# Inverse softmax sums as a diagonal in the transposing products, and half of the modulation products moved behind the SSD's residual sums

## The chip, the cores and the metric

The kernel runs on one core of a Trainium2 chip. The metric is the device time of one execution in microseconds; the time before is the median of three runs. A profiled execution gives the trace from which the rows are read. The engines are named as there: PE (TensorE matmul), PEld (its weight load), DVE (VectorE), ACT (ScalarE), POOL (GpSimd), SP (SyncE, which here only issues DMAs).

## The reference

One layer of an encoder for 1024 positions of width 1024, in fp32. The parts that the change touches are the modulation, the softmax of the chunked attention, and the places where the modulation is used:

```python
mod = (c_act @ w_ada[l] + b_ada[l])[:, None, :]
sh_m, sc_m, g_m, sh_f, sc_f, g_f = jnp.split(mod, 6, axis=-1)
h = rmsnorm(x, norm_mix_w[l]) * (1 + sc_m) + sh_m
z, xbc, dt_raw, q, k, v = jnp.split(h @ w_in[l], IN_SPLITS, axis=-1)
...
# attention: 8 heads of 64, chunks of 64, own chunk and 8 before it
scores = jnp.where(valid, scores + bias[:, None], jnp.finfo(jnp.float32).min)
p = jax.nn.softmax(scores, axis=-1).astype(v.dtype)
o = jnp.einsum('bhcqk,bckhd->bcqhd', p, vb)
...
x = x + g_m * (jnp.concatenate([y_ssd, y_att], axis=-1) @ w_out[l])
h = rmsnorm(x, norm_ffn_w[l]) * (1 + sc_f) + sh_f
x = x + g_f * conv_ffn(h, w_up[l], ffn_conv_w[l], w_down[l])
```

`mod` has 6 x 1024 = 48 x 128 values; each group of 128 is the product of a 128 x 1024 block of the transposed `w_ada` with the activated `c`. The first 16 (`sh_m`, `sc_m`) are needed before anything else, `g_m` with the output projection, `sc_f` and `sh_f` before the FFN's input, and `g_f` only in the last stage.

## The kernel before

**Numbers.** Large products are made from fp32 values split in a rounded high part and a rest (`split`: ACT writes the high part, DVE the low one), and three products of the parts (`mm3`, lines 56 to 58).

**Stages.** First the mixing norm, its 16 modulation products and the projections of head pairs 0 and 1 (to about 104 us). Then attention, four pairs of heads (`attention(0)` to `attention(3)`); the projections of pairs 2 and 3 run inside pairs 1 and 2, and the SSD's convolutions already fill PE during pair 3. Then the eight convolved groups (`conv_silu`, B, C and x), the `z` projection in two halves of eight row tiles, the SSD in eight chunks of 128 rows (`ssd_chunk`), with the output projection (`wout_tile`) of six of the eight row tiles behind it, the FFN's input (`h_raw`, `sums`), the FFN's up products, and its down products.

**Attention.** For each query tile of 128 rows and each of two heads `attn_scores` makes the scores on PE (L306), adds the bias and takes the row's extreme on DVE (L318), takes the exponential and its sums on ACT (L321), inverts the sums on DVE (L323) and scales the row block with them on DVE (L324, up to 128 x 640). `attn_pv` then turns blocks of 128 x 128 with PE transposes against the identity (L350, L353), splits the turned bank (L65 on ACT, L66 on DVE) and multiplies with the values (L361, L362). The first query tile has one block, later ones up to five: 30 blocks for a head.

**Modulation.** `mod_col` loads a block of 512 KB (L112, on SP's queue) and reduces it with the row of `c` on DVE (L113, which also has a short read-out of its sum). 16 products run in the first stage. The other 32 run with the convolutions and `z`: three for each of the eight groups, for `g_m`, `sc_f` and `sh_f` (`mods`, three buffers), and eight for `g_f` after them, in buffers that the `x` groups also use. `mod_scale` and `mod_shift` turn each column into the FFN norm's factor and offset (`affn`, `bffn`; L168, L170, L174). `row_of` turns eight columns into a row on all partitions: DVE writes a diagonal (L120), PE multiplies it with ones (L123), ACT copies (L124). It runs in the second half of `z` for `g_m` (which is folded into `w_out`, L513) and for `g_f`; the latter row goes to DRAM (`gfd`) and returns in the last stage.

**SSD and output projection.** One row tile at a time, DVE combines the chunk's parts, scales it (L705), PE turns it (L708), DVE puts it into `xs` (L709), ACT and DVE split it (`yh`, `yl`), PE multiplies with `w_out`, and DVE adds the input's rows, loaded on SP's queue (L735), to it (L747). `norm_row` then makes the FFN norm's factor as a diagonal (L759), which `h_raw` multiplies with (L797): plain fp32 products of blocks of 128 x 128, where attention has transposes.

**What sets the order.** Each engine runs its instructions, and SP its loads, in a fixed order. The framework derives it, from the code and from its own estimate of when operands are there; so the order differs from the code's and can move at places that were not edited. `issue_after(i)` keeps an instruction behind `i` in that order.

Of the kernel before, what the change touches and what calls it, by code (L numbers as in the profile page):

```python
# [10 lines left out]
F32 = mybir.dt.float32  # L11
F32R = mybir.dt.float32r
AF = mybir.ActivationFunctionType
ALU = mybir.AluOpType
# [13 lines left out]
FOLD = (0, 1, 0, 1)  # L28
PRST = 4
MTB = 3  # L30
GP, GPL = {0: (0,1), 2: (2,)}, ()
XL = (3, 4, 5, 6)
KH = NF // 2
# [12 lines left out]
def tile_block(ctx: ExitStack, tc: tile.TileContext, x, crep, pk, w_ada, w_first, w_ft, w_z,  # L46
# [39 lines left out]
    def stat(n=1):  # L86
        if stc[0] + n > 64:
            stc[0] = 0
        a = st1[:, stc[0]:stc[0] + n]
        stc[0] += n  # L90
        return a
# [16 lines left out]
        rawc[0] += 1  # L108
        return raws[:, rawc[0] % 2, 0:n]

    def mod_col(ft, t):
        nc.sync.dma_start(t, w_ada[ft])  # L112
        V.tensor_tensor_reduce(out=t, in0=t, in1=rowa, scale=1.0, scalar=0.0,  # L113
                               op0=ALU.mult, op1=ALU.add, accum_out=modc[:, ft:ft + 1])

    def row_of(cols, dst, psp, tag, bufs, ones, tmp):
        for hh in range(2):
# [45 lines left out]
    affn = const.tile([P, 8], F32, name="affn")  # L163
    bffn = const.tile([P, 8], F32, name="bffn")

    def mod_scale(dst, sc, nw, kt):
        t = stat()
        V.tensor_tensor(t, modc[:, sc + kt:sc + kt + 1], pkt[:, B_ADA + sc + kt:B_ADA + sc + kt + 1],  # L168
                        ALU.add)
        V.scalar_tensor_tensor(dst[:, kt:kt + 1], t, 1.0, pkt[:, nw + kt:nw + kt + 1],  # L170
                               op0=ALU.add, op1=ALU.mult)

    def mod_shift(dst, sh, kt):
        V.tensor_tensor(dst[:, kt:kt + 1], modc[:, sh + kt:sh + kt + 1],  # L174
                        pkt[:, B_ADA + sh + kt:B_ADA + sh + kt + 1], ALU.add)
# [120 lines left out]
    def attn_scores(p, i, bt):  # L296
        d = qk[p]
        j0 = max(0, i - 4)
        n = (i - j0 + 1) * P
        off = (j0 - (i - 4)) * P  # L300
        parts = [(0, n)] if n <= 512 else [(0, 320), (320, 320)]
        st = [s_tile(), s_tile()]
        for h in range(2):
            for pi, (a, w) in enumerate(parts):
                for ti, kn in enumerate(("kh", "kl")):
                    T.matmul(st[h][:, 512 * pi:512 * pi + w], d["q"][h][:, i * P:(i + 1) * P],  # L306
                             d[kn][h][:, j0 * P + a:j0 * P + a + w], start=ti == 0, stop=ti == 1)
        res = []
        for h in range(2):
            pt_ = p_tile()  # L310
            nm, rs = stat(), stat()
            if len(parts) == 1:
                src, bsl, dst = st[h][:, 0:n], bt[h][:, off:off + n], pt_[:, 0:n]
            else:
                src = st[h].rearrange("p (a b) -> p a b", a=2)[:, :, 0:320]
                bsl = bt[h].rearrange("p (a b) -> p a b", a=2)
                dst = pt_.rearrange("p (a b) -> p a b", a=2)
            V.tensor_tensor_reduce(out=dst, in0=src, in1=bsl, scale=-1.0, scalar=3e38,  # L318
                                   op0=ALU.add, op1=ALU.min, accum_out=nm)
# [4 lines left out]
            V.tensor_scalar(pv_, pv_, rr, None, op0=ALU.mult)  # L324
            res.append(pt_)
        return res

    def attn_pv(p, u, h, p0, p1):
# [12 lines left out]
        while done < nb:  # L341
# [5 lines left out]
            tps = tp_tile()  # L347
            for (j, c0, n), o in bank:
                if c0 == 0:
                    T.transpose(tps[:, o:o + P], p0[:, (j - lo0) * P:(j - lo0 + 1) * P], ident)  # L350
                if c0 + n == 256:
                    o1 = o + P - c0
                    T.transpose(tps[:, o1:o1 + P], p1[:, (j - lo1) * P:(j - lo1 + 1) * P], ident)  # L353
            k = ptc[0] % 3
            ptc[0] += 1
            hi, lo = pt[:, 2 * k, 0:used], pt[:, 2 * k + 1, 0:used]
# [116 lines left out]
    def mods(kt):  # L473
        mod_col(G_M + kt, mt_tile())
        mod_col(SC_F + kt, mt_tile())
        mod_scale(affn, SC_F, NFFN, kt)
        mod_col(SH_F + kt, mt_tile())
        mod_shift(bffn, SH_F, kt)

    for g in range(2):  # L480
        conv_silu(4 + g, bt_[g], th512)
# [96 lines left out]
            T.matmul(dps[:, 64 * i:64 * i + 64], m, sm["adt"], start=True, stop=True)  # L578
        A.activation(ex3, dps[:, 0:192], AF.Exp)

    for kt in range(KT):
        mod_col(G_F + kt, bcp.tile([P, S], F32, tag="rm", bufs=2, name="mt"))
    def hb(n, c):
        return sm[n][:, c * 8:c * 8 + 8].unsqueeze(2).to_broadcast([P, 8, 64])

# [42 lines left out]
    for st in range(NT):  # L628
# [103 lines left out]
    def wout_tile(st):  # L732
        xr = [wop.tile([P, 512], F32, tag="xr", bufs=2, name="xr") for _ in range(2)]
        for dh in range(2):
            nc.sync.dma_start(xr[dh], x[st * P:(st + 1) * P, halves[dh]])  # L735
        ps = [ps2b.tile([P, 512], F32, tag="wo", bufs=PB[0], name="wops") for _ in range(2)]
        for part in range(2):
            yh = wop.tile([P, 4, P], F32R, tag="yh", bufs=3, name="yh")
# [5 lines left out]
                    mm3(ps[dh], yh[:, k, :], yl[:, k, :], w[0], w[1], part == 0 and k == 0,  # L744
                        part == 1 and k == 3)
        for dh in range(2):
            V.tensor_tensor(x1[dh][:, st, :], ps[dh], xr[dh], ALU.add)  # L747
            nc.scalar.dma_start(x1d[st * P:(st + 1) * P, halves[dh]], x1[dh][:, st, :])

    dg = {}  # L750

# [541 lines left out]
```

## Time and profile before

| | |
|---|---|
| runs | 1271.11, 1270.83, 1270.24 us (median 1270.83) |
| profiled execution | 1271.27 us, span 1269.6 us, mean granted clock of PE 0.977 |
| busy over the span | PE 1189.2 us (94%), DVE 984.6 (78%), ACT 560.4 (44%), POOL 108.0 (9%) |
| 32 modulation products with the convolutions and z | 41.6 us of DVE, 512 KB each |
| 64 scalings of the probabilities | 29.6 us of DVE |

A row that groups instructions has: line, engine, operation, output<-inputs, shapes, count | busy us, mean ns of one | idle time of the engine before them and what ended it. A tile's row has the shortest, median and longest duration in ns. A row of the timeline begins with start and duration in us. PEclk is the share of the TensorE clock that was granted.

### The profile page before, as it was taken

How to read it: one execution, taken by the hardware profiler on the slowest of the kernel's cores; microseconds unless marked ns; L12 is line 12 of the kernel's file. 1: busy time of each engine (PE TensorE's matmuls, PEld its weight loads, DVE VectorE, ACT ScalarE, POOL GpSimd, SP SyncE). 2: the span in 40 equal slices, each digit the busy share in tenths (PEclk: the TensorE clock that was granted, in tenths of full speed). 3: DMA queues.
4: the chain of work that ended last, by engine and by line, in shares of the span. 5: the costliest groups of instructions: out<-in, count | busy, mean ns of one | idle time of the engine just before them, and what ended most of it. 6: DMA issues, size and time to landing. Idle time of an engine off the chain costs nothing.

```text
span 1269.6 us, 15525 instructions
## 1 busy us (share of the span) xinstructions
PE 1189.2 (94%) x5786; PEld 991.8 (78%) x5786; DVE 984.6 (78%) x1533; ACT 560.4 (44%) x917; POOL 108.0 (9%) x114
## 2 busy tenths in 40 slices
PE   5898999989979979999889999999999999999995
PEld 3686788778869868888668888888888888888884
DVE  7836666694698886764999988888988879856976
ACT  4525555573324453423744444443444445443443
POOL 1300011101220242220000000000000000000002
PEclk9998899999989989999999999999999999999998
DMA  8712111201564422112213322323322295834433
GB/s 331 258 29 65 38 51 54 62 17 34 183 226 140 166 83 67 54 55 90 69 67 124 119 80 90 110 100 124 119 81 89 79 321 208 303 110 143 158 124 132
DMA packets 57835, 150.85 MB, mean 119 GB/s; under 512 B 5793, under 2 KB 5921, under 8 KB 56353
## 3 DMA queue, kind: packets, MB, share of 16 engines
q1 hardware_dynamic: 50704, 125.49, 29.4%
q10 hardware_dynamic: 7056, 24.38, 4.8%
q8 instruction: 45, 0.74, 0.2%
q14 instruction: 30, 0.24, 0.1%
HBM read 116.56 MB, written 29.10 MB: 115 GB/s over the span
## 4 chain that ended last, share of the span: by engine, by line
PE 76%; DVE 14%; DMA 4%; ACT 3%; issue 2%; POOL 1%; SPq 0%; DVEq 0%; POOLq 0%; ACTq 0%
PE dn L57 5%; PE dn L56 5%; PE dn L58 5%; PE uY L56 5%; PE uY L58 5%; PE uY L57 5%; PE uZ L58 3%; PE uZ L56 3%; PE uZ L57 3%; PE uX L56 3%; PE uX L58 3%; PE uX L57 3%; PE acc L56 3%; PE acc L57 3%; PE acc L58 2%
## 5 line engine op out<-in xcount | busy, mean ns | idle before, releaser
L56 PE MATMUL dn<-w 128*128 128x512 f32 x308 | 111.9, 389 | 0.0
L57 PE MATMUL dn<-w 128*128 128x512 f32 x308 | 111.9, 389 | 0.0
L58 PE MATMUL dn<-w 128*128 128x512 f32 x308 | 103.3, 389 | 0.0
L65 ACT ACTIVATE w<-ya 128x1024 fp32r<-128x1024 f32 (+1 forms) x44 | 41.8, 950 | 95.6 <-PE uY L58 87.1
L764 POOL TENSOR_TENSOR st<-st,mhalf 128x1 f32<-128x1 f32 x16 | 12.4, 777 | 678.2 <-DVE st L763 678.2
L56 PEld LDWEIGHTS dn<-w 128*128 128x128 f32 x308 | 57.8, 188 | 12.1
L57 PEld LDWEIGHTS dn<-w 128*128 128x128 f32 x308 | 57.8, 188 | 12.0
L58 PEld LDWEIGHTS dn<-w 128*128 128x128 f32 x308 | 57.8, 188 | 11.9
L65 ACT ACTIVATE w<-xs 128x1024 fp32r<-128x1024 f32 (+1 forms) x44 | 41.8, 951 | 43.5 <-PE uY L58 37.5
L56 PE MATMUL s<-hth,wh 128*128 128x512 f32 x128 | 51.7, 404 | 8.8 <-DVE st L168 8.0
L66 DVE TENSOR_TENSOR pt<-tp,pt 128x512 fp32r<-128x512 f32 (+2 forms) x72 | 42.0, 595 | 17.7 <-ACT pt L65 17.2
L318 DVE CUSTOM_DVE_ANT_0 p<-s,bias 128x640 f32<-128x640 f32 (+4 forms) x64 | 40.8, 649 | 18.4 <-PE s L306 10.1
L321 ACT ACTIVATE p<-p,st 128x640 f32<-128x640 f32 (+4 forms) x64 | 44.1, 691 | 19.8 <-DVE st L318 18.7
L66 POOL TENSOR_TENSOR wl<-raws,wh 128x1024 fp32r<-128x1024 f32 x14 | 36.5, 2612 | 189.3 <-ACT wh L65 145.9
L906 DVE SCALAR_TENSOR_TENSOR a<-cv,pkt,a 128x1023 f32<-128x1023 f32 (+1 forms) x40 | 51.0, 1276 | 0.1
L57 PE MATMUL s<-htl,wh 128*128 128x512 f32 x128 | 51.0, 398 | 0.0
L58 PE MATMUL s<-hth,wl 128*128 128x512 f32 x128 | 50.9, 398 | 0.0
L66 DVE TENSOR_TENSOR w<-ya,w 128x1024 fp32r<-128x1024 f32 (+1 forms) x44 | 47.7, 1085 | 4.0 <-ACT w L65 4.0
L113 DVE CUSTOM_DVE_ANT_0 mt<-mt,rows 128x1024 f32<-128x1024 f32 x32 | 41.6, 1301 | 10.6 <-DMA mt<-in_w_ada_dram 10.6
L906 DVE SCALAR_TENSOR_TENSOR a<-cg,pkt,a 128x1023 f32<-128x1023 f32 (+1 forms) x40 | 49.6, 1276 | 0.0
L65 ACT ACTIVATE pt<-tp 128x512 fp32r<-128x512 f32 (+2 forms) x72 | 36.3, 523 | 28.8 <-PE tp L350 12.3
L66 DVE TENSOR_TENSOR w<-xs,w 128x1024 fp32r<-128x1024 f32 (+1 forms) x44 | 47.6, 1083 | 0.0
(407 smaller groups left out, 3607.6 us busy)
## 6 DMA issues: line engine op xcount, KB each, us to landing
mt<-in_w_ada_dram SPq DMA_DIRECT2D x32, 512.0 KB, 3.8
gz<-a ACTq DMA_DIRECT2D x10, 1024.0 KB, 5.3
adat<-in_w_ada_dram SPq DMA_DIRECT2D x16, 512.0 KB, 6.5
ya<-in_w_up_dram SPq DMA_DIRECT2D x10, 768.0 KB, 4.0
xs<-in_w_up_dram SPq DMA_DIRECT2D x10, 768.0 KB, 4.1
raws<-in_w_ft_dram SPq DMA_DIRECT2D x14, 512.0 KB, 3.5
gy<-a ACTq DMA_DIRECT2D x10, 512.0 KB, 2.6
qk<-in_x_dram SPq DMA_DIRECT2D x8, 512.0 KB, 6.7
```

The lines of the kernel that those rows point to most:

```text
L56: T.matmul(ps, lh, rh, start=start, stop=False, skip_group_check=more)
L57: T.matmul(ps, lh, rl, start=False, stop=False, skip_group_check=more)
L58: T.matmul(ps, ll, rh, start=False, stop=stop, skip_group_check=more)
L65: i = A.activation(hi, src, AF.Copy) if ehi is A else ehi.tensor_copy(hi, src)
L66: return i, elo.tensor_tensor(lo, src, f32(hi), ALU.subtract)
L113: V.tensor_tensor_reduce(out=t, in0=t, in1=rowa, scale=1.0, scalar=0.0, op0=ALU.mult, op1=ALU.add, accum_out=modc[:, ft:ft + 1])
L318: V.tensor_tensor_reduce(out=dst, in0=src, in1=bsl, scale=-1.0, scalar=3e38, op0=ALU.add, op1=ALU.min, accum_out=nm)
L321: A.activation(pv_, pv_, AF.Exp, scale=-1.0, bias=nm, accum_out=rs)
L764: G.tensor_tensor(r, ms, mhalf[:, 0:1], ALU.pow)
L906: V.scalar_tensor_tensor(a[:, j:S], c[:, 0:S - j], w[2 - j], a[:, j:S], op0=ALU.mult, op1=ALU.add)
```

## The change

**Diagonal.** `attn_scores` no longer scales the probabilities. It scales the identity by the inverse sums to a diagonal `dr` (128 x 128, six buffers), on ACT for the first head of a pair and on DVE for the second, and returns it with the block. `attn_pv` multiplies each block with its diagonal in a plain fp32 product in place of the transpose; the result is the turned and scaled block.

**Modulation.** `mods` keeps `g_m` and `sc_f`. The 16 products for `sh_f` and `g_f` go into the loop over the six row tiles: none at the first, three at each of the next four, four at the last. Their load stands behind the load of the tile's input rows, and their reduction behind the tile's residual sum; they have two buffers. Factor and offset are now made for all eight columns at once, and the row of `g_f` and its copy to DRAM stand behind the loop.

```diff
+DRB = 6
+LATE = (0, 0, 3, 6, 9, 12, 16)
...
-    def mod_col(ft, t):
-        nc.sync.dma_start(t, w_ada[ft])
-        V.tensor_tensor_reduce(out=t, in0=t, in1=rowa, scale=1.0, scalar=0.0,
-                               op0=ALU.mult, op1=ALU.add, accum_out=modc[:, ft:ft + 1])
+    def mod_col(ft, t, at=None):
+        sp_, v_ = at or (None, None)
+        with tc.issue_after(sp_) if sp_ else ExitStack():
+            nc.sync.dma_start(t, w_ada[ft])
+        with tc.issue_after(v_) if v_ else ExitStack():
+            V.tensor_tensor_reduce(out=t, in0=t, in1=rowa, scale=1.0, scalar=0.0,
+                                   op0=ALU.mult, op1=ALU.add, accum_out=modc[:, ft:ft + 1])
...
             rr = stat()
             V.reciprocal(rr, rs)
-            V.tensor_scalar(pv_, pv_, rr, None, op0=ALU.mult)
-            res.append(pt_)
+            dr = ptp.tile([P, P], F32, tag="dr", bufs=DRB, name="dr")
+            if h == 0:
+                A.activation(dr, ident, AF.Copy, scale=rr)
+            else:
+                V.tensor_scalar(dr, ident, rr, None, op0=ALU.mult)
+            res.append((pt_, dr))
...
-                    T.transpose(tps[:, o:o + P], p0[:, (j - lo0) * P:(j - lo0 + 1) * P], ident)
+                    k = slice((j - lo0) * P, (j - lo0 + 1) * P)
+                    T.matmul(tps[:, o:o + P], p0[0][:, k], p0[1], start=True, stop=True)
...
-                    T.transpose(tps[:, o1:o1 + P], p1[:, (j - lo1) * P:(j - lo1 + 1) * P], ident)
+                    T.matmul(tps[:, o1:o1 + P], p1[0][:, k], p1[1], start=True, stop=True)
...
     def mods(kt):
         mod_col(G_M + kt, mt_tile())
         mod_col(SC_F + kt, mt_tile())
-        mod_scale(affn, SC_F, NFFN, kt)
-        mod_col(SH_F + kt, mt_tile())
-        mod_shift(bffn, SH_F, kt)
...
-    for kt in range(KT):
-        mod_col(G_F + kt, bcp.tile([P, S], F32, tag="rm", bufs=2, name="mt"))
...
-        if st == ROWST2:
-            V.tensor_tensor(gcol[:, 8:16], modc[:, G_F:G_F + 8], gbias[1], ALU.add)
-            row_of(gcol[:, 8:16], rowa, ps1, "tp", 2, ones, rm512)
...
-    nc.sync.dma_start(gfd, rowa)
...
-            nc.sync.dma_start(xr[dh], x[st * P:(st + 1) * P, halves[dh]])
+            ld = nc.sync.dma_start(xr[dh], x[st * P:(st + 1) * P, halves[dh]])
...
-            V.tensor_tensor(x1[dh][:, st, :], ps[dh], xr[dh], ALU.add)
+            add = V.tensor_tensor(x1[dh][:, st, :], ps[dh], xr[dh], ALU.add)
             nc.scalar.dma_start(x1d[st * P:(st + 1) * P, halves[dh]], x1[dh][:, st, :])
+        return ld.ins, add.ins
...
+    late = [f + kt for kt in range(KT) for f in (SH_F, G_F)]
     for st in range(6):
-        wout_tile(st)
+        at = wout_tile(st)
         norm_row(st)
+        for ft in late[LATE[st]:LATE[st + 1]]:
+            mod_col(ft, sp.tile([P, D], F32, tag="mt", bufs=2, name="mt"), at)
+    mod_scale(affn, SC_F, NFFN, 0, 8)
+    mod_shift(bffn, SH_F, 0, 8)
+    V.tensor_tensor(gcol[:, 8:16], modc[:, G_F:G_F + 8], gbias[1], ALU.add)
+    row_of(gcol[:, 8:16], rowa, ps2b, "x", PB[1], ones, rm512)
+    nc.sync.dma_start(gfd, rowa)
```

The order moves at three places. The first is DVE during the convolutions, at the second group of C: `L414` adds the convolution's taps to it from the two score banks (`ct_2753`), and the last tap frees them for PE's next group. Before:

```order
L414 SCALAR_TENSOR_TENSOR ct_2753<-s,pkt,ct_2753 128x1022
L113 ISA mt,modc<-mt,rows 128x1024
L113 ISA modc 128x1
L174 TENSOR_TENSOR bffn<-modc,pkt 128x1
L170 SCALAR_TENSOR_TENSOR affn<-st_72,pkt 128x1
L420 SCALAR_TENSOR_TENSOR bt_2751<-th,bt_2751 128x512 x2
L113 ISA mt,modc<-mt,rows 128x1024
L113 ISA modc 128x1
L414 SCALAR_TENSOR_TENSOR ct_2753<-s,pkt,ct_2753 128x1021
```

Of the change (the tap is now L425, the modulation product L118):

```order
L425 SCALAR_TENSOR_TENSOR ct_2817<-s,pkt,ct_2817 128x1022
L118 ISA mt,modc<-mt,rows 128x1024
L118 ISA modc 128x1
L431 SCALAR_TENSOR_TENSOR bt_2815<-th,bt_2815 128x512
L118 ISA mt,modc<-mt,rows 128x1024
L118 ISA modc 128x1
L425 SCALAR_TENSOR_TENSOR ct_2817<-s,pkt,ct_2817 128x1021
```

The small additions are gone; of the modulation products, nine stand ahead of this last tap in both orders. Behind it, 23 follow before and 7 now.

The second is SP's queue from the convolutions to the output weights. Before:

```order
L112 DMA mt<-in_w_ada_dram 128x1024 x5
L532 DMA raws<-in_w_z_dram 128x520 x3
L112 DMA mt<-in_w_ada_dram 128x1024
L532 DMA raws<-in_w_z_dram 128x520
L112 DMA mt<-in_w_ada_dram 128x1024 x7
L532 DMA raws<-in_w_z_dram 128x520 x2
L511 DMA raws<-in_w_out_dram 128x512 x8
```

Of the change:

```order
L116 DMA mt<-in_w_ada_dram 128x1024 x5
L540 DMA raws<-in_w_z_dram 128x520
L116 DMA mt<-in_w_ada_dram 128x1024 x3
L540 DMA raws<-in_w_z_dram 128x520 x7
L519 DMA raws<-in_w_out_dram 128x512 x8
```

The last seven loads of z weights follow each other, and the output weights come right behind them.

The third is DVE at the end of one row tile of the SSD. Before:

```order
L747 TENSOR_TENSOR ya<-wops,xr 128x512
L747 TENSOR_TENSOR xs<-wops,xr 128x512
L705 TENSOR_SCALAR yy<-yy,st_72 128x512
L610 TENSOR_TENSOR rm<-tle_2769,adl 128x512
L763 SCALAR_TENSOR_TENSOR st_72<-st_72 128x1
L759 TENSOR_SCALAR dg<-ident,st_72 128x128
L709 TENSOR_TENSOR xs<-xps,pkt 128x512
```

Of the change:

```order
L749 TENSOR_TENSOR ya<-wops,xr 128x512
L749 TENSOR_TENSOR xs<-wops,xr 128x512
L118 ISA mt,modc<-mt,rows 128x1024
L118 ISA modc 128x1
L708 TENSOR_SCALAR yy<-yy,st_72 128x512
L118 ISA mt,modc<-mt,rows 128x1024
L118 ISA modc 128x1
L616 TENSOR_TENSOR rm<-tle_2833,adl 128x512
L766 SCALAR_TENSOR_TENSOR st_72<-st_72 128x1
L762 TENSOR_SCALAR dg<-ident,st_72 128x128
L118 ISA mt,modc<-mt,rows 128x1024
L118 ISA modc 128x1
```

Three products stand between the residual sum and the writing of the next tile into `xs` (L709 before, now L712, the next row).

More of the change, by code (lines that the diff above doesn't have):

```diff
@@ L164, in tile_block, with mod_scale, mod_shift @@
     bffn = const.tile([P, 8], F32, name="bffn")
-    def mod_scale(dst, sc, nw, kt):
-        t = stat()
-        V.tensor_tensor(t, modc[:, sc + kt:sc + kt + 1], pkt[:, B_ADA + sc + kt:B_ADA + sc + kt + 1],
+    def mod_scale(dst, sc, nw, kt, n=1):
+        t = stat(n)
+        V.tensor_tensor(t, modc[:, sc + kt:sc + kt + n], pkt[:, B_ADA + sc + kt:B_ADA + sc + kt + n],
                         ALU.add)
-        V.scalar_tensor_tensor(dst[:, kt:kt + 1], t, 1.0, pkt[:, nw + kt:nw + kt + 1],
+        V.scalar_tensor_tensor(dst[:, kt:kt + n], t, 1.0, pkt[:, nw + kt:nw + kt + n],
                                op0=ALU.add, op1=ALU.mult)
-    def mod_shift(dst, sh, kt):
-        V.tensor_tensor(dst[:, kt:kt + 1], modc[:, sh + kt:sh + kt + 1],
-                        pkt[:, B_ADA + sh + kt:B_ADA + sh + kt + 1], ALU.add)
+    def mod_shift(dst, sh, kt, n=1):
+        V.tensor_tensor(dst[:, kt:kt + n], modc[:, sh + kt:sh + kt + n],
+                        pkt[:, B_ADA + sh + kt:B_ADA + sh + kt + n], ALU.add)
     V.tensor_scalar(pkt[:, SCW:FCW], pkt[:, SCW:FCW], 0.5, None, op0=ALU.mult)
@@ L349, in attn_pv @@
                 if c0 == 0:
-                    T.transpose(tps[:, o:o + P], p0[:, (j - lo0) * P:(j - lo0 + 1) * P], ident)
+                    k = slice((j - lo0) * P, (j - lo0 + 1) * P)
+                    T.matmul(tps[:, o:o + P], p0[0][:, k], p0[1], start=True, stop=True)
                 if c0 + n == 256:
+                    k = slice((j - lo1) * P, (j - lo1 + 1) * P)
                     o1 = o + P - c0
-                    T.transpose(tps[:, o1:o1 + P], p1[:, (j - lo1) * P:(j - lo1 + 1) * P], ident)
+                    T.matmul(tps[:, o1:o1 + P], p1[0][:, k], p1[1], start=True, stop=True)
             k = ptc[0] % 3
```

## The prediction

> **What bounds the kernel now.** I read the busy table first, then the stages, then the chain of waits of the stages that the change touches. One row of the page and ten of the table by stage (busy time of each engine with its instruction count, then granted TensorE clock, DMA share, GB/s):
>
> ```profile
> PE 1189.2 (94%) x5786; PEld 991.8 (78%) x5786; DVE 984.6 (78%) x1533; ACT 560.4 (44%) x917; POOL 108.0 (9%) x114
> ...
> 104.00:150.00 46.00, 40.34 (x211) 33.25 (x212) 35.31 (x108) 27.69 (x70) 3.84 (x11) 0.89 0.20 56
> 150.00:230.00 80.00, 77.71 (x432) 66.38 (x433) 50.81 (x136) 41.52 (x94) 7.98 (x7) 0.98 0.19 53
> 230.00:260.00 30.00, 27.77 (x157) 23.47 (x156) 17.74 (x48) 16.74 (x37) 5.40 (x4) 0.94 0.22 65
> 260.00:300.00 40.00, 37.50 (x223) 31.07 (x222) 30.44 (x84) 24.38 (x55) 2.41 (x1) 1.00 0.00 1
> 300.00:335.00 35.00, 35.00 (x194) 30.25 (x192) 17.39 (x23) 9.87 (x16) 4.80 (x2) 1.00 0.25 88
> 335.00:395.00 60.00, 51.64 (x230) 42.25 (x230) 57.27 (x101) 19.99 (x31) 10.71 (x6) 0.91 0.63 212
> 395.00:430.00 35.00, 34.34 (x272) 32.68 (x271) 26.32 (x56) 11.76 (x23) 0.77 (x1) 1.00 0.54 181
> 430.00:483.00 53.00, 43.97 (x255) 37.22 (x254) 47.78 (x59) 28.18 (x64) 24.09 (x15) 0.90 0.23 80
> 483.00:585.00 102.00, 99.03 (x511) 83.68 (x510) 67.43 (x109) 35.43 (x92) 22.88 (x31) 1.00 0.20 65
> 585.00:650.00 65.00, 54.30 (x286) 44.81 (x285) 52.10 (x74) 38.20 (x62) 1.89 (x4) 0.97 0.21 73
> ```
>
> 104 to 335 us is attention: PE is busy in 218.3 of 231 us, so 12.7 are idle, and by the clock column another 8.5 (46 x 0.11 + 80 x 0.02 + 30 x 0.06) go to a slowed clock; DVE is busy in 151.7, about two thirds. 335 to 483 is convolution, z and the SSD's first products: DVE is fuller than PE in its first 60 and its last 53 us. 483 to 585 is PE again (3.0 idle of 102). The chain of waits, for 104 to 335 and for 483 to 585, says the same:
>
> ```profile
> by line: PE acc L56 10.2%; PE acc L57 9.5%; PE acc L58 9.0%; DVE p L318 8.6%; PE pv L362 5.5%; PE s L56 5.4%; DVE pt L66 5.4%; PE pv L361 5.2%; PE s L58 5.2%; PE s L57 5.1%; PE s L306 4.6%; DVE p L324 3.6%; PE tp L353 3.5%; PE tp L350 3.1%;
> by line: PE wops L56 23.0%; PE wops L57 21.7%; PE wops L58 21.1%; PE ydp L676 9.9%; PE yop L686 5.4%; PE sg L614 4.5%; PE stp L692 4.2%; DVE xs L709 3.4%; ACT yh L65 3.1%; PE xps L708 2.6%; issue 0.4%; PE xps L597 0.4%; PE xps L599 0.2%
> ```
>
> The scaling of the probabilities (L324) holds 3.6% of attention's chain, the transposes (L350, L353) 6.6%.
>
> **Part 1, the diagonal.** What goes and what comes, with the kinds of instruction that before already has: a diagonal on DVE is L759, a scaled copy of 128x128 on ACT is L609, a product of a block with a diagonal is L797.
>
> ```profile
> L324 DVE TENSOR_SCALAR p<-p,st 128x640 f32<-128x640 f32 (+4 forms) x64 | 29.6, 478 | 0.6
> L759 DVE TENSOR_SCALAR dg<-ident,st x8: 279/286/288, 488.3 to 604.6; 128x128 f32<-128x128 f32 x8
> L609 ACT ACTIVATE rm<-tle,adh x64: 384/389/407, 438.3 to 551.8; 128x128 fp32r<-128x128 f32 x64
> L353 PE MATMUL tp<-ident,p x128: 270/273/421, 116.3 to 329.0; 128*128 128x128 f32 x128
> L350 PE MATMUL tp<-ident,p x112: 270/273/435, 114.7 to 329.1; 128*128 128x128 f32 x112
> L797 PE MATMUL xps<-dg,ya x64: 270/275/377, 591.4 to 617.0; 128*128 128x128 f32 x64
> L708 PE MATMUL xps<-ident,yy x32: 270/272/317, 466.8 to 591.3; 128*128 128x128 f32 x32
> ...
> 207.96 0.27 PE L353 MATMUL tp<-ident,p 128*128 128x128 f32 x1
> 208.07 0.27 PE L350 MATMUL tp<-ident,p 128*128 128x128 f32 x1
> 208.18 0.27 PE L353 MATMUL tp<-ident,p 128*128 128x128 f32 x1
> ...
> 598.11 1.27 PE L797 MATMUL xps<-dg,xs 128*128 128x128 f32 x10
> ```
>
> DVE loses 64 x 0.478 less 32 x 0.286, that is 29.6 - 9.2 = 20.4 us; ACT gains 32 x 0.389 = 12.4 us, and it has 111 us idle in that stage. On PE the counts decide. Eight row tiles with four transposes each leave 32 records at L708: one record a transpose. Eight row tiles with eight blocks, half of them in ya, are 32 products of L797 with ya, and there are 64 records: two records a product. Records start 0.11 us apart in both cases (207.96, 208.07, 208.18; ten of L797 take 1.27 with the last one's 0.27, so 1.00/9). A transpose takes PE 0.11 us and a product 0.22; the loops make 30 blocks for each of 8 heads, which are the 128 + 112 records, and 240 x 0.11 = **26.4 us** of PE time are added to the stage where PE is fullest. That is the upper bound. The lower one goes by the chain: the transposes hold 6.6% of 231 = 15.2 us of it, or 58% of their own 240 x 0.11 = 26.4; 58% of the 26.4 added is 15.2, less what the shorter link to the product gives (3.6% of 231 = 8.3 us at 0.478, now 0.338 as the mean of 0.286 and 0.389: 2.4). That is +12.8. A lighter DVE may close some of PE's 12.7 idle us; a heavier PE puts more products on the chain. I take **+16**, near the lower end, because pair 0 (104 to 150) has 5.7 of those idle us.
>
> The Trainium skill (Perfetto Trace Analysis, section Transposes) speaks against this part: logical transposes should use the transpose and not a standard matmul, as it skips the arithmetic. By that rule alone the stage loses; the trace agrees, with 32 records against 64 for equally many blocks.
>
> **Part 2, sixteen modulation products leave the convolutions.** A product is a load of 512 KB and a DVE reduction with its read-out:
>
> ```profile
> L113 DVE CUSTOM_DVE_ANT_0 mt<-mt,rows 128x1024 f32<-128x1024 f32 x32 | 41.6, 1301 | 10.6 <-DMA mt<-in_w_ada_dram 10.6
> mt<-in_w_ada_dram SPq DMA_DIRECT2D x32, 512.0 KB, 3.8
> L113 DVE DVE_READ_ACCUMULATOR2_ANT modc<- 128x1 f32 x31 | 2.5, 79 | 0.0
> L120 DVE TENSOR_TENSOR gt<-ident,gcol 128x512 f32<-128x512 f32 x4 | 2.7, 682 | 0.0
> PE s L56 <- DVE st L168: 8.0, 1, 8.0
> 355.28 1.27 DVE L414 SCALAR_TENSOR_TENSOR ct<-s,pkt,ct 128x1021 f32<-128x1021 f32 x1
> SPq L112 <- DVE zs L549: 9.9, 4, 3.8
> ```
>
> 16 x 1.38 = 22 us leave DVE there. PE's one long wait is 8.0 us (its group's releaser stands right behind the last convolution tap, L414 at 355.28, which frees the score banks). In the order of the changed program nine products stand ahead of this tap, as before; only six small additions are gone. So this wait stays: 0.5. Behind it DVE gets free, and the queue of SP no longer holds the loads of z weights behind loads of w_ada, which wait for buffers (9.9 us there). Of 395 to 430 PE can get back at most 0.7. In 430 to 483 it loses 9.0 idle and 5.3 to the clock, and DVE, busy in 47.8 of 53, sets it: two of four diagonals of L120 leave (1.4), the other two move ahead of z's sums (1.4), and the loads of w_out no longer stand behind the last seven loads of w_ada. A part of those 9.9 us comes to it, say a fifth (2), so 5 with the two 1.4; in all **-6**, between +2 (the loads collide elsewhere) and -15 (0.7 + 9.0 + 5.3).
>
> **Part 3, they arrive behind the residual sums.** DVE has 34.6 us idle in 483 to 585 and gets 22. One row tile's end on DVE before, with the same instruction (L709) of the tile ahead, 17.3 us earlier:
>
> ```profile
> 525.14 0.69 DVE L709 TENSOR_TENSOR xs<-xps,pkt 128x512 f32<-128x512 f32 x1 [2.33 <-PE xps L708]
> ...
> 536.32 0.69 DVE L747 TENSOR_TENSOR xs<-wops,xr 128x512 f32<-128x512 f32 x1 [0.31 <-PE wops L58]
> 537.22 0.49 DVE L705 TENSOR_SCALAR yy<-yy,st 128x512 f32<-128x512 f32 x1 [0.21 <-ACT junk L756]
> 537.62 0.69 DVE L610 TENSOR_TENSOR rm<-tle,adl 128x512 fp32r<-128x512 f32 x1
> 539.01 0.16 DVE L763 SCALAR_TENSOR_TENSOR st<-st 128x1 f32<-128x1 f32 x1 [0.70 <-ACT junk L756]
> 539.84 0.29 DVE L759 TENSOR_SCALAR dg<-ident,st 128x128 f32<-128x128 f32 x1 [0.66 <-POOL st L764]
> 542.46 0.69 DVE L709 TENSOR_TENSOR xs<-xps,pkt 128x512 f32<-128x512 f32 x1 [2.34 <-PE xps L708]
> PE wops L56 <- ACT yh L65: 3.0, 5, 0.8
> ```
>
> The three products stand before L705, before L610 and before L709. The first two take 2.8 us, of which the waits of 0.21 and 0.70 cover 0.9 (the 0.66 for POOL stays); L759, which ended at 540.1, ends at 542.0. The third product's load needs the buffer of the first, free at 538.4, and 3.8 us: it starts at 542.2 and ends at 543.6, where L709 began at 542.46. L709 is what ACT's split (yh) and then PE wait for, 0.8 us a tile already (the last row), so nothing covers the 1.1. Four tiles make 4.4; the fifth, with four products, I put at the same 1.1 and no more, since PE has 10.7 idle us behind it. The gate's row moves from z to here: two products on PE and two L120 either way, 0.5 for the copy to DRAM, which now stands ahead of the w_up loads on SP. **+6**, between 0 (all fits in idle DVE time) and +22 (none does).
>
> **Sum.** 16 - 6 + 6 = +16 on the profiled execution's 1271.27 gives 1287.3; that execution lies 0.4 above the median of the runs shown (1270.83), so the forecast is **1287**. Its own range is 1279 to 1297 (part 1 between 12.8 and 21, the others 4 either way).
>
> **Rivals.**
> PE's idle time is all DVE's lateness, and a lighter DVE fills it. The idle and slowed time of 104 to 483 is 21.2 in attention, 13.8 at 335 to 395 (8.4, and 60 x 0.09) and 15.0 behind, 50 us in all; the products need 26.4 and part 3 another 6. It decides once 65% of the 50 close (32.4); at 80% the time is 1271 + 32 - 40 = 1263, faster. For it: DVE p L318 and pt L66 hold 14% of attention's chain. Against it: 300 to 335 has no idle time to fill, and nine products still precede the tap.
> All products lie on the path and part 2 gives nothing: 26.4 + 0 + 9 (half as much again in part 3) = +35, 1306. For it: PE's 94%; against it: pair 0's idle time.
> The clock stays up. Attention's slowed stretches cost 8.5; if the denser PE keeps them away, 16 becomes 7.5 and the time 1278, still slower. The Trainium skill (TensorE: Matmul & The Clock Gate, Part 4: PE-mode transpose) says that transposes do not count as activity for the gate; if so, products would. No row separates the two: the slowed windows (0.89, 0.94) also have the idle PE.
> A diagonal product costs PE no more than the transpose did (the second records are none of PE's time), and so the change gives only its gain on DVE: then part 1 is -2.4, the rest nothing (-6 + 6), and the time 1269; with more idle time closed, less. Against it: the records of L797 start 0.11 apart, so two take twice the time of one.
>
> **How the numbers follow.** Forecast 0.52, clock 0.12, all on the path 0.12, idle time filled 0.18, cheap product 0.06. A measurement here tells 0.2%, 2.5 us, from none. Faster: most of 0.18 and half of 0.06, 0.20; same: the rest of these two and the thin edge of the forecast, 0.07; slower 0.73. The range reaches halfway into both outer cases: 1267 to 1303.
>
> **What would show it.** Part 1: 480 records of the tp products with a starting distance of 0.11 us, and attention 10 to 20 us longer with PE over 96% busy. Part 2: the 8 us wait still there, the stretch that was 430 to 483 about 5 shorter. Part 3: the row tiles' period 1 us over the 17.3 shown. The forecast is wrong if attention takes no longer than 231 us, or if the wait before the x convolutions is gone.

## The result and the profile after

| | before | after |
|---|---|---|
| median of the runs | 1270.53 us (4 runs) | 1291.78 us (4 runs, 1290.61 to 1294.79) |
| ratio | | 1.017, 95% interval 1.0152 to 1.0191 |
| span of the profiled execution | 1269.6 us | 1290.9 us |

The change makes the kernel slower by 1.7%, some 21 us. The page of the changed kernel shows PE 24 us busier and DVE 18.5 us lighter over the span than before:

```profile
PE 1213.4 (94%) x6026; PEld 1022.5 (79%) x6026; DVE 966.1 (75%) x1480; ACT 571.2 (44%) x949; POOL 106.9 (8%) x114
```

To see where the 21 us arise I cut both executions at the same events: the first score product, the last product with v, the last product that feeds a convolution, the first residual sum, the first product of the FFN, and the end. The view is the table by stretch (window and its length, then busy time of PE, PEld, DVE, ACT and POOL with instruction counts, granted TensorE clock, DMA share, GB/s). The kernel before:

```profile
104.60:335.00 230.40, 217.88 (x1207) 183.98 (x1205) 151.09 (x395) 119.62 (x270) 24.43 (x25) 0.96 0.17 51
335.00:393.90 58.90, 50.54 (x221) 41.22 (x221) 56.21 (x99) 18.89 (x29) 10.71 (x6) 0.91 0.64 214
393.90:483.20 89.30, 79.61 (x533) 71.10 (x532) 75.36 (x116) 41.04 (x89) 24.86 (x15) 0.94 0.35 120
483.20:612.50 129.30, 123.70 (x669) 105.31 (x668) 81.83 (x132) 52.28 (x125) 24.77 (x35) 1.00 0.21 71
612.50:1269.60 657.10, 634.63 (x2796) 523.87 (x2796) 554.83 (x666) 284.47 (x341) 7.96 (x8) 0.99 0.37 132
```

The same table of the changed kernel:

```profile
104.00:343.10 239.10, 232.53 (x1438) 206.19 (x1437) 134.96 (x363) 130.27 (x302) 23.93 (x25) 0.99 0.16 50
343.10:398.30 55.20, 51.69 (x244) 42.57 (x243) 47.83 (x66) 21.29 (x33) 10.19 (x6) 1.00 0.50 163
398.30:480.20 81.90, 75.06 (x510) 68.61 (x509) 62.34 (x94) 37.05 (x82) 23.25 (x15) 0.94 0.20 65
480.20:633.00 152.80, 135.80 (x679) 114.51 (x677) 100.81 (x168) 53.94 (x129) 24.80 (x35) 0.93 0.36 119
633.00:1290.90 657.90, 635.78 (x2796) 524.64 (x2796) 554.73 (x666) 284.52 (x341) 7.97 (x8) 0.99 0.37 132
```

Attention is 8.7 us longer (239.1 against 230.4), the convolutions 3.7 shorter, z and the SSD's first products 7.4 shorter, the row tiles 23.5 longer, the FFN 0.8 longer, and the start 0.6 shorter: 21.3 in all. The total is close to the forecast (+16), its parts are not: the forecast had +16 in attention, -6 in the convolutions and z, and +6 in the row tiles.

**Attention.** The clock is 0.99 against 0.96, and PE is idle for 6.6 us against 12.5. The turning products are there as the prediction counted them, 224 and 256 records (this view of a line has the count, the shortest, median and longest duration in ns, first and last start):

```profile
L360 PE MATMUL tp<-dr,p x224: 270/275/377, 113.9 to 337.2; 128*128 128x128 f32 x112
...
L364 PE MATMUL tp<-dr,p x256: 270/275/377, 115.8 to 337.0; 128*128 128x128 f32 x128
```

**The row tiles.** The eight residual sums of the first half of the columns stand, in the line's view of the kernel before, between 483.2 and 597.0:

```profile
L747 DVE TENSOR_TENSOR ya<-wops,xr x8: 676/677/692, 483.2 to 597.0; 128x512 f32<-128x512 f32 x8
```

and in that of the changed kernel between 480.2 and 615.7, 135.5 us in place of 113.8:

```profile
L749 DVE TENSOR_TENSOR ya<-wops,xr x8: 676/678/692, 480.2 to 615.7; 128x512 f32<-128x512 f32 x8
```

The waits of this stage in the changed kernel (waiting engine, line and tile, what for; us in total, times, longest) show that PE now waits 13.7 us for the split of the turned tile, where the prediction quoted 3.0, and that DVE waits for loads of `w_ada`, which it did not here before:

```profile
PE wops L58 <- ACT yh L67: 13.7, 5, 3.6
...
DVE mt L118 <- DMA mt<-in_w_ada_dram: 11.5, 5, 3.3
```

The chain of waits (start, duration, what) goes through these loads in the tiles that have three products. One of them:

```profile
545.16 1.22 DVE mt L118
546.41 5.66 DMA mt<-in_w_ada_dram
552.21 1.23 DVE mt L118
553.44 0.61 DVE xs L712
554.08 0.64 ACT yh L67
554.76 0.55 PE wops L58
```

The tile's first product ends and gives its buffer back; the third product's load is issued at 546.41 and takes 5.66 us; DVE, which runs in a fixed order, cannot start the third product before 552.21 (it waits some 3 us for it), and behind it wait L712, ACT's split and PE.

That is half of it. PE stands still for 2.9 to 3.6 us in each of the four tiles, and each time, about when it starts again, the granted clock falls to half (windows of the changed kernel, columns as above):

```profile
495.00:510.70 15.70, 12.83 (x62) 10.50 (x61) 12.68 (x21) 6.15 (x17) 4.66 (x6) 1.00 0.43 146
510.70:514.10 3.40, 3.40 (x14) 3.04 (x13) 1.58 (x3) 0.60 (x1) 0.00 (x0) 0.50 0.24 99
514.10:531.20 17.10, 14.18 (x72) 11.82 (x70) 12.41 (x21) 5.04 (x16) 4.79 (x6) 1.00 0.38 124
531.20:538.00 6.80, 6.16 (x19) 5.24 (x20) 3.65 (x6) 1.71 (x3) 0.00 (x0) 0.50 0.26 77
538.00:555.10 17.10, 13.89 (x70) 11.55 (x69) 12.73 (x22) 6.02 (x17) 4.79 (x6) 1.00 0.40 127
555.10:558.50 3.40, 3.40 (x13) 3.03 (x12) 2.07 (x4) 0.40 (x2) 0.00 (x0) 0.50 0.34 133
558.50:575.60 17.10, 14.64 (x74) 12.21 (x72) 11.64 (x19) 4.26 (x12) 4.79 (x6) 1.00 0.38 124
575.60:582.40 6.80, 6.00 (x18) 5.16 (x19) 3.65 (x7) 1.75 (x3) 0.00 (x0) 0.50 0.25 77
```

In the four stretches at half clock PE is busy for 19.0 us (3.40, 6.16, 3.40 and 6.00); half of that, 9.5 us, I take as the price of the clock. The waits cost 13.7 - 3.0 = 10.7. These two make 20.2 of the 23.5 by which the stage grew. Before, the whole stage ran at 1.00.

### The profile page after: what moved, and what is told of

Same layout as the page of the kernel before. It is cut to its first block, busy times and chain, and to the rows that moved or that the text cites. A ratio compares the mean times of both kernels' runs of the same rounds, so it can differ in the third digit from the quotient of the medians.

```text
span 1290.9 us, 16008 instructions
## 1 busy us (share of the span) xinstructions
PE 1213.4 (94%) x6026; PEld 1022.5 (79%) x6026; DVE 966.1 (75%) x1480; ACT 571.2 (44%) x949; POOL 106.9 (8%) x114
## 4 chain that ended last, share of the span: by engine, by line
PE 78%; DVE 12%; DMA 4%; ACT 2%; issue 2%; POOL 1%; SPq 0%; DVEq 0%; POOLq 0%; ACTq 0%
PE dn L58 5%; PE dn L59 5%; PE dn L60 5%; PE uY L58 5%; PE uY L59 5%; PE uY L60 4%; PE uZ L59 3%; PE uZ L58 3%; PE uZ L60 3%; PE uX L59 3%; PE uX L58 3%; PE uX L60 3%; PE acc L58 3%; PE acc L59 3%; PE acc L60 3%; DVE mt L118 2%
## 5 line engine op out<-in xcount | busy, mean ns | idle before, releaser
L58 PE MATMUL wops<-woh,yh 128*128 128x512 f32 x96 | 39.9, 415 | 16.2 <-ACT yh L67 16.2
L118 DVE CUSTOM_DVE_ANT_0 mt<-mt,rows 128x1024 f32<-128x1024 f32 x32 | 43.0, 1358 | 12.8 <-DMA mt<-in_w_ada_dram 12.6
```

What stands on the lines that cost most here:

```text
L58: T.matmul(ps, lh, rh, start=start, stop=False, skip_group_check=more)
```

## The experiments

Two theories stood at the start. **Theory L:** the row tiles lose their time because two buffers hold three products, so that the third load can start only when the first product has ended. **Theory W:** the added work is the cause, that is DVE's three reductions a tile or the memory traffic of the loads, whatever the buffers. For attention, the question was what a product costs against a transpose, and whether the clock or a lighter DVE had paid part of it. Each experiment was timed against the kernel before on the same chip (1268.87 us beside the first four, 1270.64 beside the last four). The table has the stretches of above and the one ahead of them, each from one profiled execution.

| stage, us | before | after | diagonal | moved, 2 buffers | change, 3 buffers | moved, 3 buffers | products with identity | no scaling | 3,3,3,3,2,2 | 2,3,3,3,3,2 |
|---|---|---|---|---|---|---|---|---|---|---|
| ahead of attention | 104.6 | 104.0 | 102.6 | 102.3 | 104.0 | 102.7 | 103.9 | 103.9 | 104.2 | 102.7 |
| attention | 230.4 | 239.1 | 238.0 | 229.7 | 239.6 | 227.8 | 236.1 | 228.4 | 227.3 | 227.8 |
| convolutions | 58.9 | 55.2 | 59.1 | 59.1 | 57.4 | 59.1 | 63.6 | 59.2 | 59.3 | 59.4 |
| z, first products | 89.3 | 81.9 | 91.4 | 82.6 | 82.3 | 81.6 | 90.3 | 90.2 | 83.1 | 81.0 |
| row tiles | 129.3 | 152.8 | 129.6 | 151.0 | 134.2 | 135.5 | 129.6 | 130.1 | 132.0 | 134.3 |
| FFN | 657.1 | 657.9 | 656.8 | 659.5 | 660.0 | 660.0 | 656.8 | 660.1 | 656.8 | 656.7 |

### The diagonal alone

The kernel before with the first part of the change and nothing of the second:

```diff
-            V.tensor_scalar(pv_, pv_, rr, None, op0=ALU.mult)
+            dr = ptp.tile([P, P], F32, tag="dr", bufs=DRB, name="dr")
+            if h == 0:
+                A.activation(dr, ident, AF.Copy, scale=rr)
+            else:
+                V.tensor_scalar(dr, ident, rr, None, op0=ALU.mult)
...
-                    T.transpose(tps[:, o:o + P], p0[:, ...], ident)
+                    T.matmul(tps[:, o:o + P], p0[0][:, k], p0[1], start=True, stop=True)
```

> The kernel before with the diagonal alone (all 32 modulation products where they were). Theory of the traces: attention ends 8 us later, as in the change (337.2 against 329.1 for the last turned block), and PE's wait of 8.0 us ahead of the x convolutions shrinks by about 4, since DVE's work there did not move; 1274 to 1275. Rival, the prediction's price for the diagonal: +16, so 1287.

Measured: 1279.88 us, ratio 1.008 (1.0052 to 1.0101). Attention is 7.6 us longer and the stretch with z 2.1. The time lies between the two expectations and meets neither: the product costs less than the forecast's 16, and more than the trace of the change alone had suggested.

### The moved products alone

The second part of the change and nothing of the first (`LATE = (0, 0, 3, 6, 9, 12, 16)`, two buffers).

> The kernel before with the sixteen moved products alone, transposes and scaling as before. Theory of the traces: the first row tile's residual sum 7 us earlier than before (the change shows 3 earlier, with attention 8 late and about 4 of that taken up by a wait), then five row tiles 4 to 5 us longer each, +22; 1285 to 1287. Rival, the prediction's prices: -6 and +6, so 1271.

Measured: 1284.77 us, ratio 1.012 (1.0094 to 1.0143). That is 0.2 us under the range of the theory of the traces, and far from the 1271 of the prediction's prices. The stretch with z is 6.7 us shorter, the row tiles are 21.7 longer; attention and convolutions stand as before. With 1.008 and 1.012 the two parts make 1.020 where the change has 1.017: nearly a sum. The 3 us that are missing when both are there are no more than the intervals of the three ratios leave open.

### Three buffers

One size changed, in the changed kernel and in the one with the move alone:

```diff
-            mod_col(ft, sp.tile([P, D], F32, tag="mt", bufs=2, name="mt"), at)
+            mod_col(ft, sp.tile([P, D], F32, tag="mt", bufs=3, name="mt"), at)
```

> The change with three buffers for the moved products in place of two. Theory L (the third product's load): the load no longer waits for the first product of its own tile, DVE no longer waits 2.7 us for it, PE's wait per tile falls from 2.7 to under 1.5 and its clock is not lowered; the row tiles' period goes from 21.6 to between 17.5 and 18.5, and the time to 1273 to 1277. Rival W (DVE's work itself): 4.1 us of products a tile in a queue that is on the path; the buffers change nothing, 1289 to 1292.

> The moved products with three buffers, and the transposes and scaling of before. Theory L: -7 up to the first residual sum, +4 to +6 for the row tiles, so 1267 to 1269. Rival W: as with two buffers, 1285 to 1287.

Measured: the change with three buffers 1278.46 us, ratio 1.008 (1.0049 to 1.0103); the move alone with three buffers 1271.39 us, ratio 1.000 (0.9982 to 1.0023). Both lie 1.5 to 2.4 us above what theory L said, and over 10 us below theory W, which falls. The row tiles of the change take 134.2 us in place of 152.8. Their window and their wait, in the kernel of the change with three buffers:

```profile
483.30:617.50 134.20, 125.71 (x674) 105.96 (x672) 100.58 (x168) 53.44 (x127) 24.80 (x35) 1.00 0.41 135
```

```profile
PE wops L58 <- ACT yh L67: 3.9, 5, 0.8
```

DVE does the same 100.6 us of work as in the change (100.8), and the loads move the same bytes in less time (135 GB/s against 119); the wait is 3.9 where the change has 13.7, no single one above 0.8, and the clock is at 1.00 throughout. By the starts of the residual sums, the three-product tiles of this kernel are 0.2 to 0.3 us longer than before (17.5 or 17.6 in place of 17.3; 16.3 in place of 16.0), where the change with two buffers has 21.3 to 23.3. So the 18.6 us that the third buffer wins back in this stage were the price neither of DVE's reductions nor of the traffic: they were the wait for the buffer, and the clock that followed PE's standstill. The time alone does not part these two, since they came and went together.

Left over are 4.9 us in the row tiles of the change and 6.2 in those of the move alone, and three in the FFN. Of the 6.2, by the starts of the residual sums, 1.8 lie between the first sum and the sixth, 2.8 between the sixth and the eighth, and 1.6 behind the eighth. The 2.8 stand where the last tile with moved products has four of them: there the fourth load waits for the first product as the third did before, and the gate's row follows. DVE waits for that load, and PE for what stands behind it on DVE (waits from 540 to 625 us, the move with three buffers):

```profile
DVE mt L117 <- DMA mt<-in_w_ada_dram: 1.7, 1, 1.7
PE ydp L672 <- DVE th L616: 2.0, 1, 2.0
```

The three in the FFN go with an order. In the kernel with the move and three buffers, the first gate product of the FFN waits (wait view):

```profile
PE uY L57 <- DVE cg L888: 4.7, 1, 4.7
```

and in the kernel before the same one:

```profile
PE uY L56 <- DVE cg L884: 1.4, 1, 1.4
```

The order of DVE there has the two halves of `cg` one behind the other, where before and in the change a split stands between them and the first half comes earlier. No line of the FFN was edited. That the order makes the 3 us is read from these waits; no run moves it alone.

### Products with the identity, and no scaling at all

The diagonal does two things: it gives PE products for transposes, and it takes work from DVE. Two kernels do one each. The first (the line of the second block is changed likewise):

```diff
-                    T.transpose(tps[:, o:o + P], p0[:, ...], ident)
+                    T.matmul(tps[:, o:o + P], p0[:, ...], ident, start=True, stop=True)
```

> The kernel before with only its 240 transposes written as plain products with the identity; the division stays on VectorE as it was, so TensorE has the added work and VectorE has no relief. Attention (first score product to last product with v) took 230.4 us before, with 17 us of it at half clock, and 238.0 with the diagonal alone, with none at half clock. Theory P (the products themselves bring about 13 us of TensorE time and keep the clock up): at most 7 us at half clock, attention 236 to 241, the whole 1276 to 1281. Rival D (it was the lighter VectorE that closed TensorE's gaps and so kept the clock up): 10 us or more at half clock again, attention 242 to 248, the whole 1282 to 1289. If the product costs TensorE nothing: 230, and 1269.

The second leaves the division by the sums out of the computation:

```diff
             V.reciprocal(rr, rs)
-            V.tensor_scalar(pv_, pv_, rr, None, op0=ALU.mult)
```

> The kernel before without the division of the probabilities by their sums (that part of the computation is left out; 64 VectorE instructions, 29.6 us), transposes as before: VectorE is relieved and TensorE has nothing added. Theory P: the clock falls in attention as it did in the three runs with transposes (7 to 17 us at half clock), attention 225 to 229, the whole 1264 to 1269. Rival D: at most 4 us at half clock, attention 217 to 223, the whole 1256 to 1262. The shorter link was priced at 2.4 us for the diagonal, and would be worth up to 8.3 here by the chain of waits.

Measured: 1282.18 us, ratio 1.010 (1.0085 to 1.0115), and 1272.62 us, ratio 1.001 (0.9996 to 1.0029). The first total lies at the lower end of rival D's range, 1.2 us above theory P's; the second lies above both ranges. Both totals carry something from other stages, and so only the attention is read, to which the expectations had given ranges of its own: behind the products with the identity the convolutions take 4.7 us more, and in the kernel without scaling the order in the FFN is again the one with the late `cg` (660.1 against 657.1, 3.0 us). The attention stage of the diagonal alone, then of the products with the identity, then of no scaling:

```profile
102.60:340.60 238.00, 230.47 (x1439) 204.26 (x1438) 134.86 (x363) 130.28 (x302) 23.85 (x25) 1.00 0.17 50
```

```profile
103.90:340.00 236.10, 229.22 (x1422) 204.18 (x1419) 149.27 (x394) 120.88 (x270) 23.93 (x25) 0.99 0.16 50
```

```profile
103.90:332.30 228.40, 213.91 (x1207) 181.83 (x1206) 126.33 (x331) 119.47 (x270) 23.78 (x25) 0.97 0.17 51
```

With the products and an unrelieved DVE, attention takes 236.1 us, with 6.8 at half clock, and PE is idle for 6.9: the clock and the idle time are close to those of the diagonal, without any relief. With DVE 25 us lighter and transposes, PE is idle for 14.5 us, more than before, and attention takes 228.4, with 13.6 at half clock. That time lies among the four executions with transposes and the scaling other than the one before (227.3 to 229.7). Both attention times and both half-clock times lie in theory P's ranges and outside rival D's. So theory P stands and rival D falls: a lighter DVE buys nothing in attention that these executions show. The groups of DVE in attention say why (line, operation, busy us, mean ns, idle time ahead and what ended it). The row of L318 in the kernel without scaling:

```profile
L318 DVE CUSTOM_DVE_ANT_0 p<-s,bias 128x640 f32<-128x640 f32 (+4 forms) x64 | 40.8, 651 | 33.5 <-PE tp L352 14.6 <-PE s L306 13.9 <-POOL bias L376 3.7
```

and in the kernel before:

```profile
L318 DVE CUSTOM_DVE_ANT_0 p<-s,bias 128x640 f32<-128x640 f32 (+4 forms) x64 | 40.8, 649 | 18.4 <-PE s L306 10.1 <-PE tp L353 4.1 <-POOL bias L377 3.2
```

The time that DVE wins it spends waiting for PE: 33.5 us ahead of the bias addition, 28.5 of it for PE, where it was 14.2.

Behind attention a lighter DVE may be worth something: in the convolutions of the products with the identity DVE is busy for 62.0 of the 63.6 us, while the diagonal alone, with as many products and a lighter DVE, takes 59.1 there. With transposes and without scaling the stage takes 59.2, much as before, and no run separates this further.

### The products spread evenly

With three buffers, no tile needs a fourth product:

```diff
-LATE = (0, 0, 3, 6, 9, 12, 16)
+LATE = (0, 3, 6, 9, 12, 14, 16)
```

A second kernel has (0, 2, 5, 8, 11, 14, 16). Both have transposes and scaling as before.

> The moved products with three buffers and transposes as before, but handed out evenly from the first row tile on: 3, 3, 3, 3, 2 and 2 products in the six tiles, where the change has 0, 3, 3, 3, 3 and 4. With three buffers a fourth product's load can only be issued when the first product has ended; here no tile has a fourth. Theory L (the wait for that load is what the row tiles lose): the 5 us that the last of these tiles lost are gone, and the 3 us of the first gate product in the feed-forward part too, since the changed order puts its two halves of cg apart as before; 1257 to 1263 against 1268.9 for the kernel before. Rival: the first row tile has less VectorE time to spare than the others and loses 3 to 5 us, which gives 1264 to 1268. If VectorE's 22 us were themselves on the path: 1270 or more.

> The same with 2, 3, 3, 3, 3 and 2 products in the six tiles. Theory L: the same as with 3, 3, 3, 3, 2, 2 within 2 us, 1257 to 1263. Rival (the first tile is the tight one): 1 to 2 us faster than that.

Measured: 1265.92 us, ratio 0.997 (0.9957 to 0.9982), and 1266.14 us, ratio 0.998 (0.9962 to 0.999). The kernel before had 1270.64 beside them. The gain, 4.7 us, is short of the 6 to 12 expected, and 1265.92 lies in the range of the rival (1264 to 1268). But two or three products in the first tile make no difference, which decides against the rival's reason, a tight first tile. What came as expected is the FFN (656.8), and between the sixth and the eighth sum only 0.4 us are lost in place of 2.8; the row tiles still take 2.7 us more than before, 1.4 of it behind the eighth sum, and I have no cause for that. The profiled executions differ by 6.9 us and the medians by less: 3.1 of the 6.9 are in attention, which no edit touches here. The row tiles of the first, and the PE wait in them:

```profile
473.90:605.90 132.00, 125.01 (x671) 105.53 (x669) 100.25 (x167) 52.58 (x123) 26.46 (x35) 1.00 0.37 125
```

```profile
PE wops L57 <- ACT yh L66: 4.1, 5, 1.0
```

The first is 0.3% faster than the kernel before; no kernel that ran was faster, and the second is not told apart from it. The first has the half of the change that moves work, with one more buffer and no fourth product, and without the half that adds work to PE.

## Why the prediction was right or wrong

The forecast of 1287 lies 4.8 us under the result, inside its range and on the right side. That the total came so close is luck: parts 1 and 2 came out 7.3 and 5.1 us lower than forecast, and part 3 came out 17.5 higher.

**Part 1, +16, measured +8.7.** The records were as counted: 480, two a product. The term that was mis-sized is the price of the products in the stage, and both of its bounds with it. Over all executions here attention takes 227.3 to 230.4 us with transposes (mean of six 228.6) and 236.1 to 239.6 with products (mean of four 238.2): +9.6, where I had a lower bound of 12.8. By itself a product costs what the prediction said: counted from each record's start to the start of the next matmul, or to its own end where PE then stands still, the turning records hold PE for 28.1 us with transposes and 52.6 with products (means of the same executions), 24.5 more, near the 26.4. But PE's busy time in the stage rises only from 214.9 to 231.3, since that of its other matmuls falls from 186.8 to 178.7, and PE's idle time falls from 13.7 to 6.9. I had added products to the chain and left the rest of the stage as it was; the products fill part of the idle time themselves, since PE has something to do where it had waited.

Why the other matmuls count for 8.1 us less is shown in part. Half clock lengthened the stage by 5.1 us with transposes and by 2.6 with products (half the length of the half-clock stretches, means). And PE stands still 43 times with transposes and 18 times with products: the last matmul ahead of a standstill counts with its whole length, where one that is followed closely counts to the next start. An estimate from the records puts what this adds at some 7 us with transposes and 3 with products.

The credit for a lighter DVE (2.4 for the shorter link, and some idle time) was wrong in kind for attention: leaving the scaling out altogether gives no more than 2.0 against the one execution before, and nothing against the others. The chain's 3.6% for L324 (8.3 us) was no price. When that link went, DVE waited longer for PE, as the rows of L318 show.

**The rival that the clock stays up** had a part of it: in this execution the clock rose from 0.96 to 0.99 in attention. But with transposes it stands between 0.96 and 0.99 in six executions, with products between 0.99 and 1.00 in four; the execution shown before was the lowest. By the lengths of the half-clock stretches, before lost 8.5 us to it, the five other executions with transposes 3.4 to 6.8, and the four with products 0 to 3.4. The rule behind this rival, that transposes are no activity for the gate (the Trainium skill, TensorE: Matmul & The Clock Gate, Part 4: PE-mode transpose), agrees with the direction, and no run here decides it, since the two ranges touch.

**The rival that all idle time is filled** fails at the price that it named for the path: filled was half of attention's idle time, by PE's own products, and none of it by the lighter DVE.

**Part 2, -6, measured -11.1.** Taken by itself it was right: with the move alone, convolutions and z together are 6.5 us shorter, and the 8 us wait stays, as the step said. In the kernel with the move alone:

```profile
PE s L57 <- DVE ct L418: 8.1, 1, 8.1
```

What failed is the sum of the parts. With the diagonal beside it the same wait is

```profile
PE s L58 <- DVE ct L425: 3.2, 1, 3.2
```

in the changed kernel (3.5 in the one with three buffers). PE comes out of attention 8 us later, and I read part of this lateness as time that it would have waited for DVE's tap anyway. The convolutions are 3.7 us shorter and their clock is 1.00 in place of 0.91; in the change with three buffers they are 1.5 shorter, at 0.94. With the diagonal alone there are two waits of 3.4 and 2.6 in place of it, and nothing is won (59.1 us):

```profile
PE s L57 <- DVE ct L421: 3.4, 1, 3.4
PE s L57 <- DVE xst L421: 2.6, 1, 2.6
```

That it takes both, a late PE and a DVE with less to do behind it, is what these runs show; which instruction of DVE decides, I have not separated.

**Part 3, +6, measured +23.5.** This is the large error, and it lies in one step: "The third product's load needs the buffer of the first, free at 538.4, and 3.8 us: it starts at 542.2." The mechanism was seen and the sizes were not. The load takes 5.66 us here and not 3.8 (in the three-product tiles the time from issue to landing is 3.4 to 6.4, median 5.7). Loads of input rows and another modulation block are issued within 1.6 us of it; that these make it slower is likely, and no run tests it. In the view of the tile `mt` of the changed kernel from 518 to 588 us:

```profile
L118 DVE CUSTOM_DVE_ANT_0 mt<-mt,rows x9: 1215/1217/1226, 521.9 to 573.8; 128x1024 f32<-128x1024 f32 x9
...
  DMA mt<-in_w_ada_dram: 9.0, 3
...
DMA to landing us min/median/max: 3.4/5.7/6.4
```

Nine products, and each of the three third ones waits 3 us. From the step's own numbers, 5.7 in place of 3.8 would have moved the third product from 542.2 to 544.1 and its end to 545.5, 3 us behind L709 in place of 1.1. And the clock had no term at all: behind PE's standstills of 2.9 to 3.6 us it cost nearly as much again, 2.4 us a tile. With 3 us of wait and 2.4 of clock, the four tiles with three products would have come to some 22; my upper bound had the size, from another cause. The rule that idle gaps of over some 3 us bring the clock down (the Trainium skill, TensorE: Matmul & The Clock Gate, Why this matters for your kernels) agrees here: the waits of 2.9 to 3.6 us ahead of the split's product each brought a stretch at half clock, and the waits of 0.8 with three buffers none.

**What would show it.** The 480 records: yes. Attention 10 to 20 us longer: 8.7, just under it, with PE over 96% busy (232.5 of 239.1). The 8 us wait still there: no, it is down to 3.2, and the prediction had named this as one of the things that would make it wrong. The stretch of z about 5 shorter: 7.4, by my bounds. Row tiles 1 us over 17.3: no, the four with three products take 22 on average.

## What to carry to other kernels

Before a prefetch is moved, count its buffers against the largest number of loads between two points where they come free: one load too many puts a transfer, at its price in the new place, in front of everything that is queued behind its consumer. Price a stall of PE twice, as the wait and as the half-clock stretch that may follow it. A share of the chain of waits is not what removing that link brings; whether an engine's time is worth anything is better seen by what that engine itself waits for.

## What the runs showed of the hardware that I had not expected

A plain fp32 product of 128 x 128 by 128 x 128 costs about 0.22 us of PE as two records, a transpose 0.11 (in attention the starts are 0.112 and 0.109 us apart, medians); but in this stage, which also waits, 240 such exchanges cost 9.6 us and not 26.4.

The clock also falls without a long gap. In the kernel before, a stretch of attention in which PE was busy for two thirds, with no two matmul starts more than 0.96 us apart, was followed by 3.4 us at half clock:

```profile
250.00:255.60 5.60, 3.74 (x25) 2.77 (x23) 4.74 (x13) 5.58 (x14) 3.02 (x3) 1.00 0.45 129
255.60:259.00 3.40, 3.32 (x15) 3.32 (x16) 3.25 (x14) 1.93 (x9) 0.00 (x0) 0.50 0.09 37
```

In the changed kernel the same place kept its clock (1.00 over that stage behind 150 us), and in the change with three buffers it did not, with the same products (0.51 is the mean over the window's edges):

```profile
253.30:258.90 5.60, 4.09 (x30) 3.52 (x29) 3.90 (x11) 4.88 (x12) 1.59 (x3) 1.00 0.48 152
258.90:262.40 3.50, 3.50 (x19) 3.50 (x18) 1.59 (x9) 1.55 (x6) 0.00 (x0) 0.51 0.01 2
```

So one stretch of 3.4 us at half clock in attention is no property of a kernel, and a difference of that size between two profiled executions needs more than one execution of each before it is explained.

A modulation block of 512 KB takes 3.3 to 5.9 us from issue to landing in the kernel before (median 3.8) and 3.4 to 6.4 in the changed one (median 4.4; 5.7 in the three-product tiles).
